# Sixteen residual subtractions of an operand split move from VectorE to GpSimd

## The chip, the core and the metric

The kernel runs on one core of a Trainium2 chip. Time is device microseconds of one execution; the kernel before takes 2893.66 us as the median of three runs (2891.49 to 2894.02). The engines are TensorE (PE in the profile, PEld for its weight loads), VectorE (DVE), ScalarE (ACT), GpSimd (POOL) and SyncE (SP, which here only issues DMAs). Each engine works through its own list of instructions in order; semaphores make one wait for another.

## What is computed

The program is one layer of a bidirectional encoder over 2048 tokens of width 1024, in float32. What matters here is its second half:

```
h   = h + concat(y_A, y_B) @ W_out
h   = h + (silu(gate) * val) @ W_down     # gate, val = split(dwconv3(rms_norm(h) @ W_up))
h   = h + sigmoid(rms_norm(h) @ W_g) * rms_norm(p @ W_p)
out = rms_norm(h)
```

with W_out 1024 x 1024, W_up 1024 x 5632, W_down 2816 x 1024 and W_g 1024 x 1024.

## The kernel before

All large products are made with operands split in two: `hi` is the value rounded to the matmul's float32r format, `lo = raw - hi` is what is left over, and a product is the sum of three matmul groups, hi x hi, hi x lo and lo x hi. `split` (L116) makes both: ScalarE casts raw to `hi` (L120), then VectorE subtracts (L123). Where the operand also has a gain per channel, `split_g` (L125) does both steps with the gain: ScalarE at L128, VectorE at L129.

The second half of the program is one loop, `stream` (L1416), over 84 pairs of output tiles in seven blocks (`BLOCKS`): block 0 is the output projection, blocks 1 and 2 are the up-projection for the first and the second half of the tokens (22 pairs each, from i = 0 and i = 22), blocks 3 to 5 are the down-projection cut along its inner dimension (8 pairs each, from i = 44), and block 6 is the gate (8 pairs, from i = 68). In a pair, 2 x 2 blocks of a matrix product are computed by seven products instead of eight, each of 12 matmuls (9 in block 5) into a PSUM bank `fx`, `fy` or `fz`; the left operands `fw` and `fwd` are made anew for each pair (`prep_a`, `prep_b`, splits of 128x1024 and 128x512), and the seven right operands `op` stay for the whole block. They are named B11, T1, T2, B21, T3, T4 and B22, and have 4 tiles of 128x512 each (3 in block 5). B operands are plain blocks of the right matrix; T operands are sums of blocks that were made earlier and kept in DRAM.

The order of the products in pair i is: A11 x B11 into fx (copied to fy by L1547), S1 x T1 into fz, then the rest of the pair before, `rest_y` (A22 x T4, the one with `fwd`), then S2 x T2, A12 x B21, the other rest of the pair before, `rest_z` (S4 x B22), and S3 x T3. The copies and adds that empty a bank and the taps of the convolution (L1481, L1483, L1489, L1490) follow on ScalarE and VectorE; L1420 is the helper that adds.

At a change of block each operand is replaced right after its last use: `load_op` (L1275) calls `split_op` (L1285) once for each tile. B11, T1, T2, B21 and T3 are replaced in the last pair of the old block; T4 and B22 in the first pair of the new block, because `rest_y` and `rest_z` of the last pair still need the old ones. The raw tiles `opr` come by DMA on SP's queue: `op_fill` (L1261) keeps up to four loaded ahead, in a rotation of buffers (`RAWS`), six of them through blocks 2 and 3, and three, 0, 1 and 3, from the gate's T4 on. A buffer is free for the next load when the subtraction that reads it has ended.

`split_op` uses `split_g` for the B operands of blocks 2 and 6, which have a gain, and `split` for everything else. The framework lists the instructions of each engine by its own planned times, so a change of engine also changes the order of other instructions near it; a part of the end of the program alone has an order written out by hand.

In the gate, `Gate.turn` (L1833) transposes tiles `ha` of h on TensorE into banks `fs`, and ScalarE copies them to `gwr`, the raw left operands; `Gate.part` (L1856) applies the sigmoid (L1863) and the update (L1868, L1869); c12 is a copy of a bank (L1572).

GpSimd in this part runs the small row statistics of the norms (L141, L143, L1887) and, in the output projection alone, a scaling of 128x1024 tiles (L1706).

Of the kernel before, what the change touches and what calls it, by code (L numbers as in the profile page):

```python
# [60 lines left out]
class Block:  # L61
# [1223 lines left out]
    def split_op(self):  # L1285

        (blk, n, k), raw, _ = self.loaded.pop(0)
        hi, lo = self.op_place(blk, n, k)
        gain = {2: self.g2, 6: self.g3}.get(blk)
        if gain is not None and n[0] == "B":  # L1290
            kt = k + (int(n[1]) - 1) * 4
            self.split_g(raw, gain[0][:, kt:kt + 1], hi, lo)
        else:
            self.split(raw, hi, lo)
        self.op_fill()
        return hi, lo

# [745 lines left out]
```

## Time and profile before

| What | us |
|---|---|
| median of three runs | 2893.66 |
| the profiled execution's own time | 2899.36 |
| its span in the profile | 2897.6 |
| VectorE busy in 1830 to 1855 (change to block 2) | 21.55 of 25 |
| VectorE busy in 2255 to 2282 (change to block 3) | 24.90 of 27 |
| VectorE busy in 2715 to 2755 (change to block 6) | 31.03 of 40 |
| VectorE busy in 2290 to 2310 (inside block 3, for comparison) | 12.20 of 20 |

In a row of the timeline stand the start and the length in us, the engine, the line, the operation, what is written and read, the shape and how many instructions were merged; in brackets, how long the engine was idle before and what ended that. A row of the waits has engine, tile and line that waited, after the arrow what it waited for, and then the total us, the number of waits and the longest. A row with three numbers divided by strokes gives the shortest, the median and the longest of a group in ns, and the starts of its first and last in us. In a row of DMA issues the last number is the median time from issue to landing. The granted clock of TensorE in the profiled execution is 0.998 of full speed.

### The profile page before, as it was taken

Reading aid. Unit: us, or ns where it says so; the run is one execution under the profiler, and the core shown is the slowest. Engines: PE = TensorE matmul, PEld = TensorE weight load, DVE = VectorE, ACT = ScalarE, POOL = GpSimd, SP = SyncE. Lnnn points to the kernel's source line nnn. Section 1 sums busy time; section 2 is a strip of 40 time slices with the busy share of each in tenths; the row PEclk is TensorE's granted clock in tenths of the full one; section 3 lists DMA queues with packets and bytes.
Section 4 is the critical chain, followed back from the end, with each engine's and each line's share of the span. In section 5 each row is a group of like instructions: output and inputs, shape, how many; then the busy total and the mean of one; then the engine's idle time right before and its main releaser. Section 6 shows DMA issues by size and latency. Waiting matters only on the chain. (4 is left out here: it accounts for less than half of the span.)

```text
span 2897.6 us, 40196 instructions
## 1 busy us (share of the span) xinstructions
PE 2851.3 (98%) x14110; PEld 2389.4 (82%) x14110; DVE 2045.3 (71%) x3790; ACT 1506.4 (52%) x2998; POOL 209.6 (7%) x311
## 2 busy tenths in 40 slices
PE   8999999999999999999999999999999999999998
PEld 7888888788888888778788888788888788888787
DVE  7521556777777777776777877867777867676787
ACT  7311544556666666655655555655556433254765
POOL 3100000000000010024300000000000000002111
PEclk9999999999999999999999999999999999999999
DMA  6512545643333233378844554657676757476764
GB/s 188 132 59 76 163 126 162 218 155 116 112 106 104 97 106 112 124 237 274 275 142 167 191 176 142 217 180 234 226 237 211 240 181 260 157 261 213 267 219 163
DMA packets 408315, 508.94 MB, mean 176 GB/s; under 512 B 34081, under 2 KB 271665, under 8 KB 408113
## 3 DMA queue, kind: packets, MB, share of 16 engines
q1 hardware_dynamic: 408112, 506.37, 53.9%
q8 instruction: 111, 1.82, 0.2%
q14 instruction: 92, 0.75, 0.1%
HBM read 324.16 MB, written 182.12 MB: 175 GB/s over the span
## 5 line engine op out<-in xcount | busy, mean ns | idle before, releaser
L1435 PE MATMUL fz<-op,fw 128*128 128x512 f32 x1968 | 477.2, 391 | 3.4 <-ACT fw L120 3.4
L1435 PE MATMUL fy<-op,fw 128*128 128x512 f32 x1968 | 475.4, 390 | 1.5 <-ACT fy L1547 1.5
L1435 PE MATMUL fx<-op,fw 128*128 128x512 f32 x1968 | 476.0, 390 | 0.0
L1435 PEld LDWEIGHTS fz<-op,fw 128*128 128x128 f32 x1968 | 367.4, 188 | 80.4 <-ACT fw L120 4.2
L1435 PEld LDWEIGHTS fy<-op,fw 128*128 128x128 f32 x1968 | 368.5, 188 | 78.5 <-ACT fy L1547 2.2
L1435 PEld LDWEIGHTS fx<-op,fw 128*128 128x128 f32 x1968 | 368.1, 188 | 76.1 <-ACT fy L1547 0.2
L1435 PE MATMUL fy<-op,fwd 128*128 128x512 f32 (+1 forms) x984 | 238.2, 390 | 3.4 <-DVE uv L1420 3.4
L120 ACT CAST pt<-tb 128x512 fp32r<-128x512 f32 x256 | 147.0, 586 | 173.2 <-PE tb L977 172.4
L133 PE MATMUL bk<-wsp,xh 128*128 128x512 f32 (+1 forms) x768 | 234.6, 386 | 0.0
L1435 PEld LDWEIGHTS fy<-op,fwd 128*128 128x128 f32 x984 | 182.7, 188 | 42.3 <-DVE uv L1420 4.9
L919 DVE TENSOR_REDUCE mx<-bk 128x1 f32<-128x512 f32 x256 | 174.6, 684 | 41.9 <-PE bk L918 40.9
L123 DVE TENSOR_TENSOR pt<-tb,pt 128x512 fp32r<-128x512 f32 x256 | 174.0, 683 | 31.0 <-ACT pt L120 29.3
L937 ACT ACTIVATE pe<-bk,nm 128x512 f32<-128x512 f32 x256 | 174.6, 695 | 38.1 <-DVE nm L931 33.6
L989 PE MATMUL ppv<-pt,kv 128*128 128x512 f32 x512 | 189.1, 407 | 0.5 <-DVE pt L123 0.5
L133 PEld LDWEIGHTS bk<-wsp,xh 128*128 128x128 f32 x768 | 145.6, 190 | 25.2
L133 PE MATMUL bk<-wsp,xl 128*128 128x512 f32 (+1 forms) x384 | 150.8, 393 | 7.5 <-DVE xl L123 7.5
L133 PE MATMUL bk<-xh,wqk 128*128 128x512 f32 x480 | 157.2, 393 | 0.0
L977 PE MATMUL tb<-ident,pe 128*128 128x128 f32 x1024 | 151.2, 274 | 4.1 <-DVE pt L123 3.6
L990 PE MATMUL ppv<-pt,kv 128*128 128x256 f32 x512 | 145.1, 283 | 0.0
L977 PEld LDWEIGHTS tb<-ident,pe 128*128 128x128 f32 x1024 | 122.5, 141 | 24.6 <-DVE pt L123 6.5
L120 ACT CAST fw<-hraw 128x1024 fp32r<-128x1024 f32 (+1 forms) x72 | 70.2, 981 | 117.1 <-PE fx L1435 58.9
L120 ACT CAST op<-opr 128x512 fp32r<-128x512 f32 x165 | 96.0, 621 | 65.2 <-DMA opr<-tw_d 16.6
(363 smaller groups left out, 5163.0 us busy)
## 6 DMA issues: line engine op xcount, KB each, us to landing
fwr<-in_w_up SPq DMA_DIRECT2D x66, 512.0 KB, 5.4
fh<-h_d SPq DMA_DIRECT2D x48, 512.0 KB, 3.7
h_d<-fh SPq DMA_DIRECT2D x48, 512.0 KB, 4.0
s_d<-fwr SPq DMA_DIRECT2D x44, 512.0 KB, 2.6
fws<-s_d SPq DMA_DIRECT2D x44, 512.0 KB, 3.6
rw<-row_d SPq DMA_DIRECT2D x32, 512.0 KB, 5.0
tw_d<-tsum SPq DMA_DIRECT2D x60, 256.0 KB, 5.1
opr<-tw_d SPq DMA_DIRECT2D x60, 256.0 KB, 4.8
```

The source lines that it names most:

```text
L120: nc.scalar.copy(hi, src)
L123: (sub or nc.vector).tensor_tensor(lo, src, _f(hi), op=ALU.subtract)
L133: mm = lambda *a, **k: self.nc.tensor.matmul(*a, **k, skip_group_check=more)
L919: nc.vector.tensor_reduce(s.mx[:, kb:kb + 1], ps, axis=AX.X, op=ALU.max)
L937: nc.scalar.activation(s.pe[:, kb % 2], s.banks[kb], AF.Exp, bias=s.nm, scale=ASCALE, accum_out=s.rs[:, kb:kb + 1])
L977: nc.tensor.transpose(t[:, j, :], s.p[kb][:, j * P:(j + 1) * P], self.ident)
L989: mm(w.ps, vh[:, ks], pts[kb][:, j], start=kt == 0, stop=False, skip_group_check=True)
L990: mm(w.ps[:, 0], vl[:, ks], pts[kb][:, j, 0], start=False, stop=kt == NT - 1, skip_group_check=True)
L1435: nc.tensor.matmul(out, a[:, k * P:(k + 1) * P], parts[lo][:, cols], start=first, stop=lo == 1 and k == last, skip_group_check=more)
```

## The change

`split` already takes an engine for the subtraction as `sub`. `split_op` now names GpSimd in the changes to the second half of tokens (block 2), to down (block 3) and to the gate (block 6), for the operands T4 and B22:

```
@@ -1291,7 +1291,7 @@
             kt = k + (int(n[1]) - 1) * 4
             self.split_g(raw, gain[0][:, kt:kt + 1], hi, lo)
         else:
-            self.split(raw, hi, lo)
+            self.split(raw, hi, lo, sub=self.nc.gpsimd if blk in (2, 3, 6) and n in ("T4", "B22") else None)
         self.op_fill()
         return hi, lo
```

The cast to `hi`, the loads and all matmuls are the same instructions as before.

More of the change, by code (lines that the diff above doesn't have):

```diff
@@ L1293, in split_op @@
         else:
-            self.split(raw, hi, lo)
+            self.split(raw, hi, lo, sub=self.nc.gpsimd if blk in (2, 3, 6) and n in ("T4", "B22") else None)
         self.op_fill()
```

## The prediction

> **What bounds the kernel now.** First the page's busy times, then the waits of PE inside the three stretches in which the change acts (1800 to 1880, 2250 to 2340 and 2700 to 2790 us).
>
> ```profile
> PE 2851.3 (98%) x14110; PEld 2389.4 (82%) x14110; DVE 2045.3 (71%) x3790; ACT 1506.4 (52%) x2998; POOL 209.6 (7%) x311
> ...
> PE fy L1435 <- DVE uv L1420: 2.1, 2, 1.3
> ...
> PE fz L1435 <- ACT fw L120: 1.3, 1, 1.3
> PE fy L1435 <- DVE uv L1420: 0.9, 1, 0.9
> ...
> PE fz L1435 <- ACT fw L120: 2.1, 1, 2.1
> PE fs L1840 <- DMA ha<-h_d: 1.4, 1, 1.4
> ```
>
> PE (TensorE) is busy 98% of the span, so an edit that adds or removes no matmul can gain only PE's waits, and lose only by adding to them. In the three stretches these are 2.1 + 2.2 + 3.5 = 7.8 us; a change of 0.2% is 5.8 us, about what a measurement of this kernel can tell from no change. So a real gain needs three quarters of all these waits; a loss has no such bound. The sum is made as a difference against the profiled execution (span 2897.6, its own time 2899.36, so 1.8 us lie around the span). That execution is 5.7 us over the median of 2893.66, to which I add the difference.
>
> **What moves, and what it costs.** `split` makes lo = raw - hi after ScalarE's cast hi. The condition reaches T4 of blocks 2, 3 and 6 (4 each), and B22 of block 3 alone (4): B22 of blocks 2 and 6 has a gain and goes to `split_g`. So 16 subtractions go from VectorE to GpSimd; nothing else is added.
>
> ```profile
> 2231.09 3.69 DVE L123 TENSOR_TENSOR op<-opr,op 128x512 fp32r<-128x512 f32 x6
> ...
> L829 POOL TENSOR_SCALAR_AFFINE_SELECT mk<-rw x32: 634/638/1169, 651.9 to 1147.1; 128x512 f32<-128x512 f32 x32
> ...
> L1706 POOL TENSOR_SCALAR xt<-xt,rsr x16: 2851/3114/3711, 1262.7 to 1427.1; 128x1024 f32<-128x1024 f32 x16
> ```
>
> On VectorE six in a row end after 3.69 us, 0.60 apart with 0.68 for the last, so it is freed of 16 x 0.60 = 9.6 us. GpSimd has no such operation in this trace; the last of its 128x1024 rows begins at 1427, and its 7% of the span leave it free for the new work. In the gate its next instructions are the row factors of the last tile, which come after T4's four in its list and are ready later, so nothing on GpSimd waits. The nearest: 0.64 us for 128x512 with one input, and 2.85 to 3.7 for 128x1024, half of which is 1.4 to 1.9. Bounds 0.64 (second input free) to 3.2 (second input doubles 1.6); I take 1.5, nearest the row with arithmetic on real data.
>
> VectorE may be slowed meanwhile. Two places where GpSimd ran its 128x1024 operation:
>
> ```profile
> 1275.98 2.86 POOL L1706 TENSOR_SCALAR xt<-xt,rsr 128x1024 f32<-128x1024 f32 x1 [5.24 <-DMA h_d<-xt]
> ...
> 1276.98 0.69 DVE L1680 TENSOR_TENSOR yr<-yr,rb 128x512 f32<-128x512 f32 x1 [1.40 <-DMA yr<-y_d]
> ...
> 1346.90 3.64 POOL L1706 TENSOR_SCALAR xt<-xt,rsr 128x1024 f32<-128x1024 f32 x1
> ...
> 1347.82 2.25 DVE L1730 TENSOR_TENSOR nt_o<-nt_o 128x512 f32<-128x512 f32 x2
> ```
>
> In the first a two-input operation ran at its usual 0.69 inside GpSimd's. In the second two took 2.25 instead of 0.60 + 0.69 = 1.29, so 0.96 was lost, and GpSimd lost 0.8. A subtraction on GpSimd costs VectorE 0 to 0.96; I take 0.5, midway. That eats most of the 0.60 that it saves.
>
> The Trainium skill ("SBUF — State Buffer", section "Who interferes with whom") speaks against this change: a VectorE operation with two SBUF inputs and a GpSimd operation that reads SBUF lock each other out for the whole instruction. The first pair of rows disagrees, the second agrees in part; it stands as rival C.
>
> *Block 2 (1834 to 1852 us), T4.*
>
> ```profile
> 1839.93 0.68 DVE L123 TENSOR_TENSOR op<-opr,op 128x512 fp32r<-128x512 f32 x1
> 1840.54 0.69 DVE L123 TENSOR_TENSOR fwd<-fwr,fwd 128x512 fp32r<-128x512 f32 x1
> ...
> 1849.68 1.23 DVE L1490 TENSOR_TENSOR fgv<-fgv 128x1024 f32<-128x1024 f32 x1
> 1850.82 0.69 DVE L1420 TENSOR_TENSOR uv<-p,fy 128x512 f32<-128x512 f32 x1
> ...
> 1838.84 0.62 ACT L120 CAST op<-opr 128x512 fp32r<-128x512 f32 x1 [0.75 <-DMA opr<-t_d]
> ...
> 1849.00 1.75 PE L1435 MATMUL fy<-op,fw 128*128 128x512 f32 x7
> 1851.57 3.06 PE L1435 MATMUL fy<-op,fwd 128*128 128x512 f32 x12 [0.82 <-DVE uv L1420]
> ```
>
> T4's first use is the product at 1851.57, 11 us after the last subtraction at 1839.93: a slower GpSimd is covered there. PE's wait of 0.82 is for the add at 1850.82, which stands behind VectorE's queue. But the time freed before 1840.54 is lost again: ScalarE still waits for T4's loads (the cast at 1838.84) and only then casts fwd, for which VectorE must wait. From 1840.54 on VectorE has the same work as before, except that the changed build's list of instructions puts the add ahead of L1490 (1849.68 to 1850.82, 1.14): the add starts at 1850.82 - 1.14 = 1849.7 and ends near 1850.3. In the same list PE no longer has the seven matmuls of 1849.00 ahead of the product, and wants it at 1849.05. It waits about 1.1 instead of 0.82: **+0.3**. On SP the loads of B22's last two raws and of the next block's first two now wait for GpSimd, and the up weights' loads queue behind them, by 1 us or less each (1.5 against 0.6 per subtraction); they are for the pair after the next, and cost 1 us at most if that lead were gone.
>
> *Block 3 (2257 to 2282 us), T4 and B22.*
>
> ```profile
> 2260.38 0.68 DVE L123 TENSOR_TENSOR op<-opr,op 128x512 fp32r<-128x512 f32 x1
> ...
> 2267.16 0.68 DVE L1420 TENSOR_TENSOR ug<-ug,fz 128x512 f32<-128x512 f32 x1
> ...
> 2277.73 0.68 DVE L123 TENSOR_TENSOR op<-opr,op 128x512 fp32r<-128x512 f32 x1
> ...
> 2265.67 0.62 ACT L120 CAST op<-opr 128x512 fp32r<-128x512 f32 x1 [0.92 <-DMA opr<-in_w_down]
> ...
> 2267.88 1.24 ACT L1481 ACTIVATE fgv<-ug,fcw 128x1024 f32<-128x1024 f32 x1 [0.16 <-DVE ug L1420]
> 2269.03 1.03 ACT L120 CAST fw<-hraw 128x1024 fp32r<-128x1024 f32 x1
> ...
> 2267.53 1.29 PE L1435 MATMUL fy<-op,fwd 128*128 128x512 f32 x5
> 2270.11 1.20 PE L1435 MATMUL fz<-op,fw 128*128 128x512 f32 x4 [1.28 <-ACT fw L120]
> ...
> 2280.11 2.88 PE L1435 MATMUL fz<-op,fw 128*128 128x512 f32 x12
> ```
>
> Eight subtractions on GpSimd from 2260 on end at 2260 + 8 x 1.5 = 2272, sooner than VectorE's last (2277.73 + 0.68), and B22 is first used at 2280.11. What decides is the cast at 2269.03 for product S1. In the changed list ScalarE does B22's last cast (2265.67; its load waits for GpSimd's second subtraction, 2260 + 3.0 = 2263.0, where it waited for VectorE's, next after 2260.38), the tap activation (2267.88, 1.15 to the next), c22's copy (0.5, as the gate's row below) and then this cast. The activation waits for the add at 2267.16, which ends at 2267.84 less the four T4 subtractions ahead of it (2.4 us) plus four times 0 to 0.5: at 2265.4 to 2267.4. After 2265.67 + 0.5 or 2267.4, then 1.15 + 0.1 + 0.5 + 1.05, the cast ends, and S1 starts, at 2269.0 to 2270.2. The changed list has S1 ahead of the five matmuls of 2267.53, so PE waits 1.5 to 2.7 instead of 1.28: +0.2 to +1.4, I take **+0.9**, the upper half, since VectorE has no gap there to take up a delay.
>
> *Block 6 (the gate, 2726 to 2745 us), T4.*
>
> ```profile
> 2727.14 1.89 DVE L123 TENSOR_TENSOR op<-opr,op 128x512 fp32r<-128x512 f32 x3
> ...
> 2733.22 0.75 DVE L1868 SCALAR_TENSOR_TENSOR pj<-pj,gt,gate 128x512 f32<-128x512 f32 x1 [2.60 <-ACT gate L1863]
> ...
> 2736.77 0.68 DVE L123 TENSOR_TENSOR fwd<-gwr,fwd 128x512 fp32r<-128x512 f32 x1
> ...
> 2728.52 0.43 SPq L1271 DMA_DIRECT2D opr<-tw_d  x1
> ...
> opr<-tw_d SPq DMA_DIRECT2D x60, 256.0 KB, 4.8
> ...
> 2729.73 0.59 ACT L1572 COPY c<-fy 128x512 f32<-128x512 f32 x1 [0.38 <-PE fy L1435]
> ...
> 2730.83 1.28 ACT L1863 ACT_TABLE_LOAD   x1
> 2732.49 0.69 ACT L1863 ACTIVATE gate<-fx,gt 128x512 f32<-128x512 f32 x1 [0.38 <-PE fx L1435]
> ...
> 2734.30 0.62 ACT L120 CAST op<-opr 128x512 fp32r<-128x512 f32 x1 [1.12 <-DMA opr<-tw_d]
> ...
> 2740.01 1.05 ACT L120 CAST fw<-gwr 128x1024 fp32r<-128x1024 f32 x1 [1.01 <-DVE gwr L1391]
> ...
> 2741.03 1.39 PE L1435 MATMUL fz<-op,fw 128*128 128x512 f32 x5
> ```
>
> T4's fourth raw tile reuses the first one's buffer, so its load (2728.52) waits for the first subtraction: 2727.8 on GpSimd, as on VectorE. It lands about 2733. What moves is the queue behind it: in the changed list its cast stands ahead of c12's copy (2729.73), the copies out of fs, the table load and the sigmoid, not behind them. ScalarE then stands until 2733.2; behind the cast (0.6) the copy ends at 2734.3, the copy out of fs (0.5) at 2734.8, the table load (1.28) at 2736.1 and the sigmoid (0.69) at 2736.8, and VectorE's pj, which waits for it, starts at 2736.9 instead of 2733.22. On VectorE fwd, the differences L1390 and L1391, and with them the cast at 2740.01 come 2.0 later (fwd at 2738.8 instead of 2736.77: pj and two adds, 0.6 each, are ahead of it). On SP, T4's load now stands ahead of loads of ha, and B22's third, which waits for T4's last subtraction (2733.8 + 1.5), ahead of those of hb, pj and the next ha. I cost these at nothing: the next pair's transposes and last adds use them, behind the same late cast; without that cover it is another load's 4.8 us at most. PE wants S1 about 2741 and gets it at 2743: **+2.0**; 0 if the load lands 2 us sooner, 3.5 with GpSimd at 3.2 us.
>
> Sum: 0.3 + 0.9 + 2.0 = **+3.2 us, 2896.9**.
>
> **The rivals.**
> A, the forecast: queues put in another order cost more than the freed VectorE gives. 0.48; its own range 2893 to 2900.
> B, faster: VectorE's relief reaches PE. The waits of 0.82 and 1.28 vanish and the gate's load lands in time: -2.1, 2891.6. For it: VectorE is busy almost without a gap in both stretches. Against: both late operations hang on ScalarE's order too. 0.22.
> C, slower: GpSimd's subtraction blocks VectorE for its whole 1.5 us. Place: the four subtractions ahead of the add at 2267.16, 4 x (1.5 - 0.6) = 3.6 later on top of the before, with 1.2 for the filler lost; +2 in block 2, +3.5 in the gate: about +10, 2904. It decides from about 1.0 us of blocking per subtraction. For it: 2.25; against: 1276.98. 0.22.
> D, GpSimd needs over 2.5 us each: 8 x 2.5 = 20 us from 2260 reaches 2280.11, where PE then waits for B22; at 3.2 it is 5.5 us there, +3.5 in the gate, so 2903. 0.08.
> By the Trainium skill ("GPSIMD Engine Reference", section 3.1) a float32 tensor_tensor of 2048 columns takes 4497 ns, an estimate of 1.1 us for 512; by it D falls away and the sum hardly moves.
>
> **How the numbers follow.** Slower by over 0.2% (above 2899.4): most of C and D (0.23) and A's upper end (0.05): 0.28. Faster (below 2887.9) only if nearly every wait goes, within B: 0.04. The rest is 0.68. The range runs from just below B to C: 2889.5 to 2905, with about a tenth left out on either side.
>
> **What would show it.** In the profile after: 16 rows of L123 on POOL near 1.5 us; VectorE's busy time about 10 us less its stretching; PE's wait at the add for uv about 1.1 (block 2), at fz for fw 1.5 to 2.7 (block 3), and a new one of about 2 at fz in the gate, behind a ScalarE cast waiting for tw_d. I am wrong if PE's waits in the three stretches shrink, if rows of VectorE grow by more than 0.96, or if PE waits for B22 near 2280.

## The result and the profile after

The kernel after takes 2907.43 us, the median of six runs (2905.13 to 2910.5), against 2894.88 us for six runs of the kernel before (2891.49 to 2898.03). The ratio is 1.0041 with a 95% interval of 1.003 to 1.0051, so the change costs some 12 us. The forecast was 2896.9 with a range up to 2905.0: it is wrong, and the time lies above the range.

The medians lie 12.5 us apart, but the spans of the two profiled executions only 6.1 (that of after, 2903.7 with an own time of 2905.44, is one of its quicker ones, and that of before was slower than all six above). Most of the 6.4 between the two figures is there before the change first acts: at block 2 the same matmul of PE stands 4.3 us earlier in the trace of after than in that of before. The losses are therefore read as shifts between the two traces inside the three stretches.

First the busy times on the page of the kernel after, then PE's waits in the three stretches (1800 to 1880, 2250 to 2345, 2700 to 2800 us) and the group of the moved subtractions:

```profile
PE 2853.9 (98%) x14110; PEld 2389.8 (82%) x14110; DVE 2047.8 (71%) x3774; ACT 1507.4 (52%) x2998; POOL 234.9 (8%) x327
```

```profile
PE fy L1435 <- DVE uv L1420: 2.7, 2, 1.6
...
PE fz L1435 <- ACT fw L120: 3.3, 1, 3.3
PE fz L1435 <- DVE fw L123: 3.2, 1, 3.2
...
PE fz L1435 <- ACT fw L120: 2.6, 2, 1.7
PE fy L1435 <- DVE p L1420: 1.3, 1, 1.3
```

```profile
L123 POOL TENSOR_TENSOR op<-opr,op x16: 1290/1710/2278, 1830.2 to 2735.5; 128x512 fp32r<-128x512 f32 x16
```

VectorE has lost 16 instructions (3790 to 3774) worth 9.6 us and yet is busy 2.5 us longer, so its other rows grew by about 12 us. PE's wait in block 3 for ScalarE's part of `fw` rose from 1.3 to 3.3, and a wait of 3.2 for VectorE's part came on top, which in the kernel before never came last.

The timeline of the kernel after at the change to down, VectorE and GpSimd, with ScalarE's cast for S1:

```profile
2255.35 14.97 POOL L123 TENSOR_TENSOR op<-opr,op 128x512 fp32r<-128x512 f32 x8 [418.08 <-ACT op L120]
...
2256.45 1.56 DVE L1483 SCALAR_TENSOR_TENSOR fgv<-uv,fcw,fgv 128x1024 f32<-128x1024 f32 x1 [0.69 <-ACT fgv L1481]
...
2258.53 1.72 DVE L1483 SCALAR_TENSOR_TENSOR fgv<-uv,fcw,fgv 128x1024 f32<-128x1024 f32 x1
2260.17 1.77 DVE L123 TENSOR_TENSOR fwd<-hraw,fwd 128x512 fp32r<-128x512 f32 x1
2261.87 0.67 DVE L1420 TENSOR_TENSOR ug<-ug,fz 128x512 f32<-128x512 f32 x1
2262.47 1.18 DVE L1390 TENSOR_TENSOR hraw<-hraw 128x512 f32<-128x512 f32 x1
2263.68 1.64 DVE L1391 TENSOR_TENSOR hraw<-hraw 128x512 f32<-128x512 f32 x1
2265.24 2.28 DVE L1483 SCALAR_TENSOR_TENSOR fgv<-ug,fcw,fgv 128x1024 f32<-128x1024 f32 x1
2267.45 1.75 DVE L1408 TENSOR_TENSOR hraw<-hraw 128x512 f32<-128x512 f32 x1
2269.12 2.28 DVE L123 TENSOR_TENSOR fw<-hraw,fw 128x1024 fp32r<-128x1024 f32 x1
...
2265.35 2.00 ACT L120 CAST fw<-hraw 128x1024 fp32r<-128x1024 f32 x2 [0.97 <-DVE hraw L1391]
```

While GpSimd subtracts (until 2255.35 + 14.97 = 2270.3) rows of VectorE grow: 128x512 from 0.69 to up to 1.77, 128x1024 from 1.22 or 1.28 to up to 2.28. The add of L1420 keeps its 0.67; one of its inputs is a PSUM bank (fz). The excess over the usual lengths is 0.28 + 0.44 + 1.08 + 0.49 + 0.95 + 1.00 + 1.06 + 1.06 = 6.4 us, 0.8 for each subtraction, which VectorE itself had done in 0.60. GpSimd pays too: 14.97 / 8 = 1.87 each, against 1.29 where nothing collides. The two engines take strict turns. The eight subtractions, one by one, end at 2256.92, 2259.16, 2261.39, 2263.10, 2264.77, 2266.44, 2268.65 and 2270.32; the eight rows that grew end 0.54 to 0.55 (128x512) or 1.08 (128x1024) after them, one behind each. So a row that begins during a subtraction waits for its end, and the growth, 0.28 to 1.08, is what was left of it less 0.14 to 0.20. Each following subtraction in turn ends 1.12 to 1.16 after the row that it met.

PE in the same stretch, after and then before:

```profile
2260.23 2.88 PE L1435 MATMUL fx<-op,fw 128*128 128x512 f32 x12
2266.45 1.78 PE L1435 MATMUL fz<-op,fw 128*128 128x512 f32 x4 [3.34 <-ACT fw L120]
2271.46 3.78 PE L1435 MATMUL fz<-op,fw 128*128 128x512 f32 x8 [3.23 <-DVE fw L123]
2275.04 3.87 PE L1435 MATMUL fy<-op,fwd 128*128 128x512 f32 x12
2278.74 2.89 PE L1435 MATMUL fy<-op,fw 128*128 128x512 f32 x12
```

```profile
2264.81 2.88 PE L1435 MATMUL fx<-op,fw 128*128 128x512 f32 x12
...
2274.66 2.88 PE L1435 MATMUL fy<-op,fw 128*128 128x512 f32 x12
```

Between these two products lie the same 36 matmuls in both kernels (A11 x B11, S1 and `rest_y`). From the start of the one to the start of the other it is 9.85 us before and 18.51 after: **8.66 us lost**, the "stretch" of the table below. The waits are 5.3 of it (3.34 + 3.23 - 1.28). The rest is in the matmuls, 4 in 1.78 us where before took 1.20, 8 in 3.78 and 12 in 3.87 where 12 take 2.88. The windows of the kernel after show why (window, its length, then busy us and count of PE, PEld, DVE, ACT and POOL, PE's granted clock, DMA share, GB/s):

```profile
2267.00:2272.00 5.00, 1.77 (x4) 0.91 (x4) 5.00 (x5) 0.83 (x2) 3.32 (x2) 0.50 0.27 91
2272.00:2278.00 6.00, 6.00 (x17) 4.71 (x16) 5.15 (x10) 2.11 (x2) 0.00 (x0) 0.58 0.92 261
2278.00:2285.00 7.00, 7.00 (x32) 5.77 (x32) 5.87 (x10) 0.74 (x2) 0.00 (x0) 1.00 0.98 360
```

In the two windows of the slow matmuls PE's granted clock is 0.50 and 0.58, and 1.00 again from 2278 on; before, it is 1.00 throughout this stretch.

The gate, in the timeline of the kernel after:

```profile
2734.79 0.62 ACT L120 CAST op<-opr 128x512 fp32r<-128x512 f32 x1 [2.52 <-DMA opr<-tw_d]
...
2738.42 0.75 DVE L1868 SCALAR_TENSOR_TENSOR pj<-pj,gt,gate 128x512 f32<-128x512 f32 x1 [3.90 <-ACT gate L1863]
...
2744.64 1.20 PE L1435 MATMUL fz<-op,fw 128*128 128x512 f32 x4 [0.87 <-ACT fw L120]
...
2747.36 0.72 ACT L128 ACTIVATE op<-opr,gt 128x512 fp32r<-128x512 f32 x1 [2.28 <-DMA opr<-in_w_ple_gate]
...
2748.11 0.75 DVE L129 SCALAR_TENSOR_TENSOR op<-opr,gt,op 128x512 fp32r<-128x512 f32 x1 [1.60 <-ACT op L128]
...
2749.52 3.02 PE L1435 MATMUL fy<-op,fwd 128*128 128x512 f32 x12 [1.33 <-DVE p L1420]
```

ScalarE stands 2.52 us for T4's fourth tile with the sigmoid behind it, and pj waits 3.90 for the sigmoid; by this chain S1 comes 0.87 late. The other wait, 1.33 for the add of p, has another cause: the add stands in VectorE's list right behind the low part of B22's fourth tile (2748.11), and that waits for a load. The load was issued at 2741.71 and ScalarE could use the tile at 2747.36, 5.65 us later, where before it was 3.83 (2738.18 to 2742.01). It stands on SP's queue behind loads of hb, pj and ha (issued from 2737.18 to 2738.61), which stand behind B22's third tile, which waits for GpSimd's last subtraction of T4; that these loads slowed it is likely and was not tested. Together PE loses **2.2 us** where before it waited for nothing. In block 2 PE waits up to 1.6 us for the add `uv` where it waited 0.82, and the lead of 4.3 us over the trace of before shrinks to 3.6: **0.7** lost. Together 0.7 + 8.7 + 2.2 = 11.6 us, against 12.5 between the medians; the other parts of the two traces differ by about a microsecond either way.

### The profile page after: what moved, and what is told of

Read it like the earlier page. It is cut to its first block, busy times and chain, and to the rows that moved or that the text cites. A ratio compares the mean times of both kernels' runs of the same rounds, so it can differ in the third digit from the quotient of the medians.

```text
span 2903.7 us, 40200 instructions
## 1 busy us (share of the span) xinstructions
PE 2853.9 (98%) x14110; PEld 2389.8 (82%) x14110; DVE 2047.8 (71%) x3774; ACT 1507.4 (52%) x2998; POOL 234.9 (8%) x327
## 3 DMA queue, kind: packets, MB, share of 16 engines
q8 instruction: 111, 1.82, 0.2%
```

## The experiments

Eleven kernels were run: nine change or extend the one line of the change, two (e5, e6) PE's list in the kernel after. "Stretch" is the time from A11 x B11 to S2 at the change to down, as above (9.85 before). The ratio is an estimate of its own and need not be the quotient of the two medians; they differ most in e8 (6.8 us by the medians, 4.3 by the ratio).

| Kernel | median, and that of before beside it | ratio (95%) | stretch |
|---|---|---|---|
| after | 2907.43, 2894.88 | 1.0041 (1.003 to 1.0051) | 18.51 |
| e1 down only | 2904.25, 2896.66 | 1.0029 (1.002 to 1.0039) | 17.68 |
| e2 both engines | 2905.35, 2896.66 | 1.003 (1.0018 to 1.0042) | 19.41 |
| e3 write only | 2897.21, 2896.66 | 1.0 (0.9991 to 1.0009) | 9.92 |
| e4 one input | 2899.22, 2896.66 | 1.0007 (0.9998 to 1.0017) | 10.80 |
| e5 PE kept busy | 2908.29, 2898.28 | 1.0031 (1.0022 to 1.004) | 15.69 |
| e6 rest first | 2906.79, 2898.28 | 1.0028 (1.0017 to 1.0039) | 13.74 |
| e7 up and gate only | 2902.03, 2898.28 | 1.001 (1.0001 to 1.002) | not touched |
| e8 B22 only | 2905.11, 2898.28 | 1.0015 (1.0006 to 1.0025) | 15.10 |
| e9 gate only | 2896.76, 2895.4 | 1.0005 (0.9994 to 1.0017) | not touched |
| e10 gate, three of four | 2896.84, 2895.4 | 1.0005 (0.9994 to 1.0016) | not touched |
| e11 gate, write only | 2895.14, 2895.4 | 1.0001 (0.9989 to 1.0012) | not touched |

**Where: block 3 or the other two (e1, e7).** e1 moves the eight subtractions of block 3 alone, e7 only T4 of blocks 2 and 6.

```
e1:  sub=self.nc.gpsimd if blk == 3 and n in ("T4", "B22") else None
e7:  sub=self.nc.gpsimd if blk in (2, 6) and n == "T4" else None
```

> Only the eight subtractions of block 3 (T4 and B22 at the change to down) go to GpSimd. If block 3 holds the loss, as the two traces read (PE's waits at fz 3.3 + 3.2 us, then matmuls at half clock, against one wait of 1.3 before), the time is 8 us over the kernel before, two thirds of the whole change. If the loss is spread over all three places as predicted (0.3, 0.9, 2.0 and the rest unseen), it is +1 to +4 us.

> Only T4 of block 2 and of the gate (4 + 4) go to GpSimd. From the trace of the changed kernel: PE's wait for uv in block 2 grows by 0.7 us, and the gate's waits by 2.2 (0.9 at fz, 1.3 at fy, behind ScalarE's cast that waits for T4's fourth load): +3 us, within 1.5. If the gate's late product is VectorE's stretching, its first late operation there is fwd or the differences, longer than 0.69.

The parts add up: 0.29% and 0.10% against 0.41% for all. In e7 PE's longest wait in block 2 is 1.55 us, and in the gate it waits 1.1 for the add of p, behind B22's fourth load as in after; the expected 0.9 at fz is not there. Seven tenths of the loss are in block 3, where e1 loses 17.68 - 9.85 = 7.8 us in the stretch and 8.4 (0.0029 x 2896.66) in the whole.

**What: the new order, or two engines at once (e2, e3, e4).** In e2 VectorE makes all low parts as before, and GpSimd repeats the eight subtractions of block 3 into a scratch tile; the lists of PE, VectorE, ScalarE and SP are those of before. In e3 the low parts of T4 and B22 in block 3 are left out: GpSimd fills their tiles with zeros and reads nothing; PE's and VectorE's lists are those of e1. In e4 they are replaced by raw x 0.001, an operation with one input; the lists are those of e1 as well.

```
e2: +    self.nc.gpsimd.tensor_tensor(self.at("s2", [P, SB], BF16, "junk"), raw, _f(hi), op=ALU.subtract)
e3: +    self.nc.scalar.copy(hi, raw)
    +    self.nc.gpsimd.memset(_f(lo), 0.0)
e4: +    self.nc.scalar.copy(hi, raw)
    +    self.nc.gpsimd.tensor_scalar(lo, raw, 0.001, None, op0=ALU.mult)
```

> Kernel before, with VectorE still making every lo; GpSimd makes the eight subtractions of block 3 a second time into a scratch buffer. The lists of PE, VectorE, ScalarE and SP are those of the kernel before. Contention theory (GpSimd's reads hold up VectorE's operations with two SBUF inputs, about 0.8 us for each subtraction): those operations grow by about 6 us in all between 2255 and 2275, PE's wait for S1 at fz grows from 1.3 to 5 us or more, and the time by 4 to 9 us. Order theory (the loss comes from the changed lists): VectorE's durations may grow but the time stays within 2 us of before, since no list has changed.

> As the run with block 3 alone, but GpSimd writes zeros into the eight lo tiles instead of subtracting (the lo part of T4 and B22 of block 3 is left out): it reads nothing from SBUF. PE's and VectorE's lists are the same as with the subtractions. Contention theory: no operation of VectorE grows, PE's wait for S1 is at most that of before (0 to 1.5 us), time -2 to +1 us. Order theory: PE's waits at fz stay at 5 us or more and the time at +6 to +9.

> As the run with block 3 alone, but GpSimd's eight operations read one SBUF tile (lo = 0.001 x raw, so lo of T4 and B22 of block 3 is replaced). Lists of PE and VectorE as with the subtractions. Contention by reads shared between the engines: VectorE grows by about half as much, 2 to 4 us, time +1 to +5. A lock for the whole GpSimd operation: as much stretch for each us that GpSimd is busy as with two inputs. Order theory: +6 to +9 as with the subtractions.

The timelines of e2, e3 and e4 in turn:

```profile
2256.32 14.47 POOL L1296 TENSOR_TENSOR junk<-opr,op 128x512 bf16<-128x512 f32 x8 [829.35 <-ACT op L120]
...
2264.54 3.46 DVE L123 TENSOR_TENSOR op<-opr,op 128x512 fp32r<-128x512 f32 x2
...
2274.21 2.08 PE L1437 MATMUL fz<-op,fw 128*128 128x512 f32 x4 [6.47 <-ACT fw L120]
```

```profile
2262.57 0.68 DVE L123 TENSOR_TENSOR fwd<-hraw,fwd 128x512 fp32r<-128x512 f32 x1
...
2266.70 1.20 PE L1439 MATMUL fz<-op,fw 128*128 128x512 f32 x4 [0.81 <-ACT fw L120]
2268.25 2.11 PE L1439 MATMUL fz<-op,fw 128*128 128x512 f32 x8 [0.35 <-DVE fw L123]
```

```profile
2256.35 13.29 POOL L1296 TENSOR_SCALAR op<-opr 128x512 fp32r<-128x512 f32 x8 [827.98 <-DMA opr<-tw_d]
...
2261.30 1.10 DVE L123 TENSOR_TENSOR fwd<-hraw,fwd 128x512 fp32r<-128x512 f32 x1
```

With the order of before and the eight subtractions beside it, everything is lost (19.41): VectorE needs 3.46 for two subtractions that took 1.28, and S1 waits 6.47. With the order of after and nothing read by GpSimd, nothing is lost (9.92, and fwd takes 0.68). So the order is neither needed for the loss nor enough for it; GpSimd's reads are. Since nothing but the cast reads the raw tiles in e3, their loads come sooner there too, but that is not what saves the time: from A11 x B11 to the end of S1's low part it is 11.17 us in after and 5.20 in e3, and the 6.0 between them are what the rows of VectorE grew. One input less costs VectorE 0.42 on the fwd row (0.68 to 1.10) where the subtraction cost 1.09, and the stretch grows by 0.95 only.

The Trainium skill ("SBUF — State Buffer", section "Who interferes with whom") has just this pattern: VectorE operations with two SBUF inputs contend with GpSimd operations that read SBUF, not with those that only write. e2, e3 and the untouched row of L1420 agree. The prediction has from the same place that the two lock each other out for the whole instruction, and for the subtractions the rows bear that out too: in e2 as in after, each row that met a subtraction ends 0.54 to 0.55 or 1.08 to 1.09 us behind its end. The growth stays under the 1.29 of a lone subtraction because the row begins when part of it is done. Beside e4's operation with one input there is no such rule: its rows grow by 0 to 0.42.

e3 also says what the relief of VectorE is worth by itself: eight subtractions fewer on VectorE and no collision bring 9.92 in place of 9.85 and a ratio of 1.0. In the order of instructions that the framework gives, there is no gain in this place that a better engine could collect, and no version that beats the kernel before came out of these runs.

**The slow matmuls (e5, e6).** Both begin from the kernel after. e5 gives PE 24 matmuls into an unused bank at the change to down, 12 ahead of S1 and 12 after S1's first four. e6 puts the 12 of `rest_y` ahead of S1.

```
e5: +            fill = 12 if i == NUP + 1 else 0
    +            for _ in range(fill):
    +                nc.tensor.matmul(s.spare, s.ops["A11"][0][:, 0:P], self.xop["B11"][0][0], start=True, stop=True)
    -            prod(s.z, s.ops["S1"], "T1")
    +            prod(s.z, s.ops["S1"], "T1", fill=fill, spare=s.spare)
e6: +            if i == NUP + 1:
    +                rest_y(prev)
```

> The changed kernel with 24 matmuls more on PE, whose result nothing reads: 12 ahead of product S1 of the second pair of block 3, 12 between its first 4 and its last 8 matmuls, about 2.7 us each time, inside PE's two waits of 3.3 and 3.2 us. Clock theory (the matmuls after the waits are slow because PE stood idle): the granted clock stays near 1.00 from 2262 to 2278 instead of 0.50 to 0.58, the 24 matmuls after the waits take 6 us instead of 9.4, and the time falls 1.5 to 3.4 us below the changed kernel. If idling has nothing to do with it, the slow matmuls stay and the time is that of the changed kernel (+-1).

> The changed kernel with one product moved on PE: A22 x T4 (12 matmuls, 2.7 us, ready early) goes ahead of S1 in the second pair of block 3 instead of behind it; all else in PE's and ScalarE's lists is the same. Contention theory: S1's operand stays late, because VectorE is stretched as before; PE's wait ahead of S1 falls from 3.3 to about 0.6 us, the second of 3.2 stays, time 2.7 to 5 us below the changed kernel (more than 2.7 if the clock holds), still 3 us or more above the kernel before with the other two places. If PE's order alone made the loss, all of the 8 us of block 3 goes.

A window and the timeline of e5, then the timeline of e6:

```profile
2267.00:2272.00 5.00, 3.85 (x17) 2.84 (x17) 5.00 (x4) 1.25 (x2) 3.83 (x2) 1.00 0.21 59
```

```profile
2273.94 2.89 PE L1435 MATMUL fy<-op,fwd 128*128 128x512 f32 x12
```

```profile
2278.24 3.07 PE L1435 MATMUL fz<-op,fw 128*128 128x512 f32 x8 [3.13 <-DVE fw L123]
2281.11 3.60 PE L1435 MATMUL fy<-op,fw 128*128 128x512 f32 x12
```

In e5 the granted clock stays at 1.00 and the same 12 matmuls of `rest_y` take 2.89 instead of 3.87; the stretch is 2.8 shorter than after's, though PE does more in it. In the whole time the ratios 1.0031 and 1.0041 have intervals that overlap, so the expected fall of 1.5 to 3.4 us is neither shown nor excluded there, and the size of this term rests on the traces. e6 has 0.92 (ahead of `rest_y`, for ScalarE's copy c) in place of the first wait and keeps the second, 3.13 for `fw`, and the slow matmuls behind it: the two waits are separate.

**B22 alone (e8).**

```
sub=self.nc.gpsimd if blk == 3 and n == "B22" else None
```

> Only B22 of block 3 (4 subtractions) goes to GpSimd; PE's list is that of the kernel before. Contention theory: they run when VectorE works on S1's operand, four operations of VectorE are stretched by about 1 us, PE's wait at fz grows from 1.3 to 3 us or more, time +1 to +4. Relief theory: VectorE has four operations less, three of them after S1; no change or -1.

The timeline of e8:

```profile
2265.13 3.49 DVE L123 TENSOR_TENSOR op<-opr,op 128x512 fp32r<-128x512 f32 x2
...
2274.87 2.08 PE L1435 MATMUL fz<-op,fw 128*128 128x512 f32 x4 [5.07 <-ACT fw L120]
```

Four subtractions collide with what is left of VectorE's queue and cost 5.25 in the stretch. PE's list is that of before here, which again sets the new order aside.

**The gate: the order, or collisions (e9, e10, e11).** e9 moves T4 of the gate alone; e10 only three of its four tiles, so that ScalarE's cast of the fourth stays behind the sigmoid; in e11 the low parts are left out and their tiles filled with zeros, ScalarE's and VectorE's lists as in e9.

```
e9:  sub=self.nc.gpsimd if blk == 6 and n == "T4" else None
e10: sub=self.nc.gpsimd if blk == 6 and n == "T4" and k > 0 else None
e11: +    self.nc.scalar.copy(hi, raw)
     +    self.nc.gpsimd.memset(_f(lo), 0.0)
```

> Only the four T4 subtractions of the gate go to GpSimd; blocks 2 and 3 are as before. Both theories: ScalarE's T4 cast behind the load of tw_d stands ahead of the sigmoid, waits about 2.5 us, pj starts about 4 us after VectorE is free, and PE waits about 2.2 us in two places (fz about 0.9, fy about 1.3, with 0.7 either way) in the first pair of the gate, where before has none; time 2 us over before, which one round can't tell from nothing. It is the kernel that the next two are held against.

> GpSimd makes the last three of T4's four low parts in the gate, VectorE the first, so that ScalarE's last T4 cast stays behind the sigmoid as in before. Theory order (the cast that waits for the load, with the sigmoid queued behind it, costs PE 2.2 us): no wait of over 0.5 us at fz or fy in the gate's first pair, the sigmoid near its old place (0 to 1 us late). Theory collision (GpSimd's subtractions stretch VectorE by 1.07 us each, and that costs PE): three collisions, so 1.5 us or more of PE's 2.2 us remain.

> The four low parts of T4 in the gate are left out: GpSimd fills their tiles with zeros and reads nothing; ScalarE's and VectorE's lists are those of the gate alone on GpSimd. Theory order: the cast of T4's last tile still waits 2 us or more for tw_d ahead of the sigmoid, and PE still waits 1.5 to 2.7 us in the gate's first pair. Theory collision: no row of VectorE is stretched, PE's new waits shrink to 0.5 us or less.

Their timelines in turn, with the issue of the fourth tile's load (SPq) in e9 and e11:

```profile
2726.67 0.32 SPq L1271 DMA_DIRECT2D opr<-tw_d  x1
...
2730.50 0.62 ACT L120 CAST op<-opr 128x512 fp32r<-128x512 f32 x1 [2.13 <-DMA opr<-tw_d]
...
2740.34 1.21 PE L1435 MATMUL fz<-op,fw 128*128 128x512 f32 x4 [0.49 <-ACT fw L120]
...
2745.24 3.02 PE L1435 MATMUL fy<-op,fwd 128*128 128x512 f32 x12 [1.35 <-DVE p L1420]
```

```profile
2727.02 1.55 DVE L123 TENSOR_TENSOR op<-opr,op 128x512 fp32r<-128x512 f32 x1
...
2733.38 0.62 ACT L120 CAST op<-opr 128x512 fp32r<-128x512 f32 x1 [0.32 <-DMA opr<-tw_d]
```

```profile
2721.67 0.32 SPq L1271 DMA_DIRECT2D opr<-tw_d  x1
...
2725.17 0.62 ACT L1295 CAST op<-opr 128x512 fp32r<-128x512 f32 x1 [0.43 <-DMA opr<-tw_d]
```

e9 brings the two new waits back (0.49 + 1.35 = 1.8). e10 has more growth by collisions than e9 (1.55 for 0.69 and 1.55 for 1.22, against 1.82 for 1.22 alone) and not one of these waits: the cast stands behind the sigmoid again, and the add of p ahead of B22's fourth tile. So in the gate it is the order, not the collisions. e11 by itself came out as the collision theory had it and missed the order theory's forecast: with the order of e9 the cast waits only 0.43, and PE for nothing. The reason lies in the loads. Nothing but the cast reads the first raw tile there, so the buffer is free sooner: the fourth load is issued 0.64 us after the first tile's cast began (2721.03), in e9 2.02 after it (2724.65). So the order costs only together with loads that wait for GpSimd's subtractions. The whole times of these three can't be told from before.

## Why the prediction was wrong

- *What bounds.* Right: all of the loss is in PE's waits and in matmuls behind them, and no gain came from VectorE's relief.
- *GpSimd's subtraction, 1.5 us within 0.64 to 3.2.* Right: 1.29 alone, 1.71 the median, 1.87 in block 3. Rival D (over 2.5 each) fell: B22 is complete at 2270.3, ahead of its use.
- *"A subtraction on GpSimd costs VectorE 0 to 0.96; I take 0.5, midway."* This is the step that failed. In block 3 it is 0.8 on average and up to 1.08, more than the 0.60 that it saves. Both of the prediction's pairs of rows stood beside the same operation with one input (L1706): the undisturbed row of 1276.98, and the two rows at 1347.82, whose 0.96 is 0.48 for each. e4 shows that one input costs much less (0 to 0.42 a row) than a subtraction with two, so neither pair showed the price, and a midpoint between them had no row of its own.
- *Block 3, +0.9.* Measured 8.7, with three faults in it. The forecast let S1's cast follow ScalarE's own queue; the cast in fact waited 0.97 for the difference L1391, which together with L1390 had grown by 1.44. So the wait came to 3.34 against 1.5 to 2.7. It charged four subtractions, those ahead of the add, when all eight collide with the chain through S1's low part (2269.12). That part ended last for S1's other eight matmuls, a second wait of 3.23 that was nowhere in the sum. And the slow matmuls, 3.4 us (8.66 less 5.29 of longer waits), were not in it either.
- *Block 2, +0.3.* The place and the swapped order were right; the size was 0.7.
- *The gate, +2.0.* The size, 2.2 in the trace, is right partly by luck. The forecast chain is there (the load of tw_d ahead of the sigmoid, then pj, then S1), but it costs 0.87, not 2.0, and in e7 nothing at fz. The other 1.33 comes by SP's queue, by way of B22's fourth tile, and of the delays on that queue the prediction says "I cost these at nothing".
- *The rivals.* What happened is rival C by its mechanism, given 0.22; its threshold ("from about 1.0 us of blocking") was high, as 0.8 on average was enough. Its price of +10 is made of 4.8, 2 and 3.5, where 8.7, 0.7 and 2.2 were measured: block 3 was low for the same two reasons as the forecast's (only four subtractions, no term for the clock), and the other two places were high. B (VectorE's relief reaches PE) fell, in e3 even without the collisions.
- *What would show it wrong.* "if rows of VectorE grow by more than 0.96": they did, by up to 1.08.

## What to carry to other kernels

Before work goes from VectorE to GpSimd, go through VectorE's rows in the window in which GpSimd will run, and count those with both inputs in SBUF: here each collision cost 0.28 to 1.08 us, 0.8 on average, for a saving of 0.60, and rows with an input from PSUM cost nothing. Follow the delay through every part that the waiting product needs (here hi by ScalarE, lo by VectorE), not only the part that comes last today. Follow the loads as well: a buffer whose release moves to another engine moves every load that is queued behind its own. And where a forecast wait of PE grows past some 2 us, add the matmuls that may follow it at a lower clock: here 3.4 us beside 5.3 of longer waits.

## What the hardware showed that was not expected

The clock. A wait of PE may cost more than its length. Two equal waits of the gate, the first in the timeline of the kernel before, the second in that of e9, which has nothing of the change before this point:

```profile
2720.45 1.20 PE L1435 MATMUL fz<-op,fw 128*128 128x512 f32 x4 [2.12 <-ACT fw L120]
...
2722.01 2.00 PE L1435 MATMUL fz<-op,fw 128*128 128x512 f32 x8
```

```profile
2717.86 1.20 PE L1435 MATMUL fz<-op,fw 128*128 128x512 f32 x4 [2.20 <-ACT fw L120]
...
2719.82 3.19 PE L1435 MATMUL fz<-op,fw 128*128 128x512 f32 x8
```

The eight matmuls behind the first take 2.00 us, those behind the second 3.19, at a granted clock of 0.66 from 2718 to 2723. In the thirteen traces there are thirteen such waits of 1.89 to 2.39 us in down and the gate after which PE runs on; behind five of them matmuls are slow. Behind waits of up to 1.72 none is; behind those of over 3 us some always are, in e1 only behind the second of two (3.59 and 3.81). The Trainium skill ("TensorE: Matmul & The Clock Gate", section "HAM oscillation — how this bites in real kernels") warns of idle gaps over about 3.4 us; here gaps of two thirds of that cost PE its clock at times. Its account (the same page, "Part 1: The HAM clock gate") of a window that runs freely, so that the place of a gap in it counts, agrees with the clock that the traces record.

In each trace the granted clock changes only at whole multiples of 3.41 us from its other changes. In after it falls at 519.19 and at 2266.82, which is 512 times 3.4133 apart, and it stays at half for 10.24 us, three times 3.41; in e1 it stays there for two, in e9 for one. Cut into windows on that grid, the wait of before is divided, 1.50 us in one window and 0.62 in the next, while that of e9 falls whole into one (2.20 of 3.41). Over the thirteen traces, the first and the last 20 us aside, all 20 windows in which PE was idle for 1.87 us or more were followed by one at half clock, and none with 1.77 or less was; between the two, 8 of 17 were. So a little more than half a window of idling was enough here. It may also be part of why executions of one kernel differ by several us, which was not tested.

The price of a collision depends on what GpSimd reads, not only on how long it runs: a row of VectorE with two SBUF inputs loses up to 1.08 us to a subtraction (1.29 alone), up to 0.42 to an operation with one input that itself took 1.66 us beside VectorE, and nothing to a fill. Why one input costs less than half was not tried. Nor is it only rows with two inputs that wait: a copy of 128x2 with one SBUF input took 1.26 us instead of 0.16 at 1830.30 in after, ending 0.02 behind the subtraction that it met, and 1.27 in e7.
